# A two-layer mixer: the second weight fold as three fp32r products, its splits on ScalarE and GpSimd, and the first stage's loads and context work put in another order

## The chip, the cores and the metric

The kernel runs on one core of one Trainium2 chip. The time is the device time of one execution in microseconds (us); the times shown are medians of several runs. One more execution was profiled, and every row quoted in this document is from such a profile. The engines are called PE (TensorE, matrix products), DVE (VectorE), ACT (ScalarE), POOL (GpSimd) and SP (SyncE, which issues nearly all DMA transfers). Each engine works through its own list of instructions in a fixed order and waits where an operand isn't there yet.

## The reference

`x` is 1024 tokens of 1024 features, `ctx` 256 tokens that come before them, `c` and `c_ctx` conditioning vectors. Layer 0 (even) and layer 1 (odd) are:

```python
shift, scale, gate = split(silu(c) @ mod_w[l] + mod_b[l], 3)
hx = rmsnorm(x, norm_g[l]) * (1 + scale) + shift
# even layer; hc is ctx under the same weights with c_ctx
va, vg, ga, xb, gb = split(hx @ w_in, 5)
y_a = silu(layernorm(conv31(va * sigmoid(vg)))) * silu(ga)
y_b = rglru(conv4(xb), start=state of rglru(conv4(hc @ w_xb))) * silu(gb)
x = x + gate * (concat(y_a, y_b) @ w_out)
# odd layer
u, g = split(hx @ w_in, 2)
d = multiscale_pool(u)                      # 4 groups of 512 features
y = concat([d_g @ w_grp[g] for g in range(4)]) * od_scale
x = x + gate * ((y * silu(g)) @ w_out)
```

At the end stands one more rmsnorm. The pooling is linear in the tokens, so `u`'s weights and `w_grp` can be multiplied ahead of time: `wu[g] @ grp[g]`, one product of weights for each of the four groups. The kernel calls this a fold.

## The kernel before, in words

Everything is held transposed, features on the 128 partitions and tokens along the free dimension: a tensor of 1024 features is eight tiles (k = 0 to 7) of 128 x 1024. A large product is taken in split precision: an fp32 operand becomes a high part (an fp32r cast on ACT) and a low part (source minus high, on DVE or POOL; `split`, L101), and three products high*high, high*low, low*high are summed in PSUM (`mm3_steps`, L128, and `mm3_fixed`, L487, which also ties the order by hand). A matmul of plain fp32 does without the split; the trace shows it as two records.

The first stage (L293 to L466) does many things at once, and the change lies in it:

- Two of the four folds, `fold_whole` (L267): group matrices `grp[g]` are loaded to two tiles, then four times a tile `wu` is loaded, eight plain fp32 matmuls are made with it (two sums of four), ACT copies each sum (`fo`) and SP stores it to DRAM (`wfold`). `fold_some(n)` (L318) moves on by n steps of this, so the folds are laid between other work.
- The modulation vectors of layer 0: `modulation(k)` (L340) loads two tiles of `mod_w` and DVE multiplies each with silu(c) (`cL`) and silu(c_ctx) (`cC`), summing along the row into `m0`; the products themselves go to a tile `junk` that nobody reads. Two of the eight k are made on PE instead (`mod_row`).
- The rsqrt of x: ACT squares, DVE and POOL add, PE sums over the partitions (L188 to L208).
- `modulate(k)` (L371): DVE multiplies x with the scale and the rsqrt, which lies in PSUM (L375), ACT casts x plus shift to `h0h`, DVE makes `h0l` (L379).
- The context: `ctx_load` (L411) squares on ACT and adds on POOL in pieces of 256 columns, `ctx_scale` (L416) multiplies with the rsqrt on DVE, `modulate_ctx` (L383) applies scale and shift on POOL and splits with POOL.

The stage after it (L705 on) begins with weight tiles `xb0` and `vg0`, the product xb for the context (`xbc`) and for x, and then for each j the products vg, va, xb of the next j, and the gates of the recurrence. Here DVE, ACT, POOL and PE each follow an order written by hand (`on`, L471). The four PSUM buffers of `pm` are taken in turn by vg, va, xbc and the twelve gate products.

Tiles come from pools with a fixed number of buffers per tag; who takes a buffer waits for its last user. Tag `t` has four buffers of 512 columns, the weight tags `wr`, `wh`, `wl` two each of 1024. Where the program doesn't tie the order, a planner lays the instructions of each engine out at build time. In this first stage the loads on SP are tied one after the other (`load`, L108, by `chain`); the stores of the folds are put between them.

Of the kernel before, what the change touches and what calls it, by code (L numbers as in the profile page):

```python
# [15 lines left out]
P = 128  # L16
# [39 lines left out]
def body(ctx, tc, xT, ctxT, cc, ccol, modT, modW, win, gw, wout, wu, grp, wg, wo1, small, edge, ident, outT):  # L56
# [18 lines left out]
    def dtile(name, dt=F32):  # L75
        return dpool.tile([P, S], dt, tag="d", name=name)
# [24 lines left out]
    def split(src, hi, lo, eng):  # L101
        return (nc.scalar.copy(hi, src),  # L102
                eng.tensor_tensor(out=lo, in0=src, in1=hi.bitcast(F32), op=sub))  # L103
# [4 lines left out]
    def load(out, src):  # L108
        with ExitStack() as lctx:
            if chain[0] is not None:  # L110
                lctx.enter_context(tc.issue_after(chain[0].ins))
            d = nc.sync.dma_start(out, src)
            if chain[0] is not None:
                chain[0] = d

    def wload(src, name, eng, n=D, out=None):
        raw = wpool.tile([P, n], F32, tag="wr", name=f"wr_{name}")
        load(raw, src)
        if out is None:
            hi = wpool.tile([P, n], F32R, tag="wh", name=f"wh_{name}")  # L120
            lo = wpool.tile([P, n], F32R, tag="wl", name=f"wl_{name}")
        else:
            hi, lo = out(f"wh_{name}", F32R), out(f"wl_{name}", F32R)
        split(raw, hi, lo, eng)
        return hi, lo
# [15 lines left out]


    sm = base.tile([P, N_SM], F32, name="sm")
    nc.sync.dma_start(sm, small)
    eg = base.tile([P, 4 * 16], F32, name="eg")
    nc.sync.dma_start(eg, edge)

    def col(o, n=1):
        return sm[:, o : o + n]
# [19 lines left out]
    nc.scalar.activation(sa, sa, AF.Exp, scale=-1.0)  # L169
    nc.vector.tensor_scalar(out=sb, in0=sa, scalar1=2.0, scalar2=None, op0=add)  # L170
    nc.vector.reciprocal(sb, sb)
    nc.vector.tensor_tensor(out=sz, in0=sa, in1=sb, op=mult)
    nc.vector.tensor_tensor(out=sb, in0=sz, in1=sz, op=mult)
    nc.vector.memset(sa, 1.0 / 17.0)
    for n in range(7, -1, -1):
        nc.vector.tensor_tensor(out=sa, in0=sa, in1=sb, op=mult)
        nc.vector.tensor_scalar(out=sa, in0=sa, scalar1=1.0 / (2 * n + 1), scalar2=None, op0=add)
    nc.vector.tensor_tensor(out=sa, in0=sa, in1=sz, op=mult)
    nc.vector.tensor_scalar(out=sb, in0=lam, scalar1=-1.0, scalar2=0.0, op0=mult, op1=ALU.max)
    nc.vector.scalar_tensor_tensor(out=sa, in0=sa, scalar=2.0, in1=sb, op0=mult, op1=add)  # L180
    nc.vector.tensor_scalar(out=chalf, in0=sa, scalar1=4.0, scalar2=None, op0=mult)
    nc.vector.tensor_scalar(out=cneg, in0=sa, scalar1=-8.0, scalar2=None, op0=mult)


    def rstd(acc, eps, name, wn=0):
# [78 lines left out]
            yield  # L264


    def fold_whole(g, out_tile, g_tile, w_tile):  # L267
        gs = []
        for i in range(2):
            raw = g_tile(f"graw_{g}_{i}")  # L270
            load(raw, grp[g, i])
            gs += [raw[:, 0:H], raw[:, H:D]]
        yield
        for kp in range(KT // 2):
            w = w_tile(f"wu_{g}_{kp}")
            load(w, wu[g, kp])
            for s in range(2):
                ps = psum(f"fold_{g}_{kp}_{s}")
                for i in range(4):
                    kc = slice(i * 2 * P + s * P, i * 2 * P + (s + 1) * P)  # L280
                    nc.tensor.matmul(ps, w[:, kc], gs[i], start=(i == 0), stop=(i == 3))  # L281
# [15 lines left out]
    hh, hl, ch, cl = [], [], [], []  # L297
    with ExitStack() as sctx:
        fpool = sctx.enter_context(tc.tile_pool(name="fpool", bufs=6))
        gpool = sctx.enter_context(tc.tile_pool(name="gpool", bufs=4))  # L300
        spool = sctx.enter_context(tc.tile_pool(name="spool", bufs=1))

        def fo_tile(name):
            return fpool.tile([P, H], F32, tag="fo", name=name)

        def g_tile(name):
            return gpool.tile([P, D], F32, tag="g", name=name)

        raws = [0]

        def raw_tile(name):
            tag = ("wr", "wh", "wl")[raws[0] % 3]
            raws[0] += 1
            return wpool.tile([P, D], F32, tag=tag, name=name)
# [15 lines left out]
        def sumsq(acc_, v, n, first, name, eng):  # L330
            if first:
                nc.scalar.activation(acc_[:, :n], v, AF.Square)
            else:
                q = ttile(name)
                nc.scalar.activation(q[:, :n], v, AF.Square)
                eng.tensor_tensor(out=acc_[:, :n], in0=acc_[:, :n], in1=q[:, :n], op=add)

        junk = spool.tile([P, D], F32, name="junk")

        def modulation(k):  # L340
            for m in (k, KT + k):
                raw = dtile(f"mod0_{m}")
                load(raw, modT[0, m])
                mod_tile(m0, 0, m, raw, (cL, cC), junk)
            mod_scale(m0, a0, 0, k)

# [36 lines left out]
        def modulate_ctx(k):  # L383
            i, q4 = k // 4, k % 4
            cs = slice(q4 * C, (q4 + 1) * C)
            nc.gpsimd.tensor_scalar(out=cx[i][:, cs], in0=cx[i][:, cs], scalar1=a0[:, 1, k : k + 1],
                                    scalar2=m0[:, 1, k : k + 1], op0=mult, op1=add)
            ch.append(cth[i][:, cs])
            cl.append(ctl[i][:, cs])
            if q4 == 3:  # L390
                split(cx[i], cth[i], ctl[i], nc.gpsimd)

        def x_load(k):
            t = xtile(f"x_{k}")
            load(t, xT[k])
            xs.append(t)
            for h in range(2):
                sumsq(acc[h], t[:, HALF[h]], H, k == 0, f"xsq_{k}_{h}", nc.vector if h else nc.gpsimd)

        for i in range(2):  # L400
            chain[0] = nc.sync.dma_start(cx[i][:1], cc[i : i + 1])
        load(ccv, ccol)
        nc.scalar.activation(ccv, ccv, AF.Silu)
        load(idx, ident)
        for i, t in enumerate((cL, cC)):
            ps = banks(f"c_{i}", i)
            for h in range(2):
# [2 lines left out]
                nc.scalar.activation(t[:, HALF[h]], ps[h], AF.Silu, scale=float(D))  # L410
        def ctx_load(i):  # L411
            load(cx[i].rearrange("p (k n) -> p k n", n=C), ctxT[4 * i : 4 * i + 4].rearrange("k p n -> p k n"))
            for q4 in range(4):
                sumsq(accc, cx[i][:, q4 * C : (q4 + 1) * C], C, i + q4 == 0, f"csq_{i}_{q4}", nc.gpsimd)

        def ctx_scale():  # L416
            rstd(accc, eps_r, "c")
            for i in range(2):
                v = cx[i].rearrange("p (k n) -> p k n", n=C)
                nc.vector.tensor_tensor(out=v, in0=v, in1=accc.unsqueeze(1).to_broadcast([P, 4, C]), op=mult)  # L420

        def ctx_split(i):
            for k in range(4 * i, 4 * i + 4):
                modulate_ctx(k)
# [72 lines left out]
    def all_of(steps):  # L497
        for _ in steps:
            pass
# [127 lines left out]
    with ExitStack() as actx:  # L627
# [1175 lines left out]
```

## Time and profile before

| | |
|---|---|
| time, median of 3 runs | 1308.26 us (1306.17 to 1309.4) |
| the profiled execution's own time | 1307.88 us |
| its span, first to last instruction | 1306.1 us |
| granted TensorE clock, mean | 0.994 |
| first matmul of the first fold | 12.4 us |
| first matmul of the xb product | 82.2 us |
| HBM read, written | 136.72 MB, 44.04 MB |

A timeline row reads: start in us, duration in us, engine, line, operation, tile written<-tiles read, shapes, count (x3: three in a row, the duration is that of all); in brackets the idle time of the engine just before and what ended it. A row of a group ends with: busy us, mean ns of one | idle us before. Buffer numbers are left out of tile names. A busy PE is not PE at its peak, as ends of matmuls are modelled: the distance from one start to the next is what one costs.

### The profile page before, as it was taken

The numbers are of one execution on the slowest core, as the hardware profiler recorded it, in microseconds if no ns is written. First come the engines' busy times: TensorE is split into PE (matmuls) and PEld (weight loads), VectorE is DVE, ScalarE is ACT, GpSimd is POOL, SyncE is SP. The second block draws the span as 40 slices with busy tenths as digits, with TensorE's granted clock in tenths as the row PEclk, the third lists the DMA queues.
The fourth block names the chain that finished last, engine by engine and source line by source line (L and its number), as shares of the span: only waits on it lengthen the run. The fifth ranks groups of instructions, "written<-read, shape, count | busy, mean of one in ns | idle before, by whom it ended". The sixth has DMA issues, their size and how long they took to land.

```text
span 1306.1 us, 15709 instructions
## 1 busy us (share of the span) xinstructions
PE 1276.3 (98%) x5600; PEld 1023.0 (78%) x5600; DVE 1137.2 (87%) x1764; ACT 632.0 (48%) x919; POOL 352.1 (27%) x179
## 2 busy tenths in 40 slices
PE   8999999999999999999999999999999999999995
PEld 3468888888888887788887887788778888778784
DVE  7969999999999989969789758998999987887876
ACT  5333656566656623227435346734343344644642
POOL 2153655576657712443210022000000000000002
PEclk9999999999999999999999999999999999999998
DMA  9934112121112233443555356244334334868723
GB/s 358 360 97 169 57 41 65 41 73 45 61 44 86 65 105 116 152 147 103 169 188 187 127 194 189 86 137 153 109 104 134 113 121 129 284 209 289 265 65 129
DMA packets 82867, 181.80 MB, mean 139 GB/s; under 512 B 7778, under 2 KB 27618, under 8 KB 82788
## 3 DMA queue, kind: packets, MB, share of 16 engines
q1 hardware_dynamic: 74340, 176.60, 40.2%
q10 hardware_dynamic: 8448, 4.20, 1.1%
q8 instruction: 44, 0.72, 0.2%
q14 instruction: 35, 0.29, 0.1%
HBM read 136.72 MB, written 44.04 MB: 138 GB/s over the span
## 4 chain that ended last, share of the span: by engine, by line
PE 68%; DVE 10%; DMA 6%; ACT 4%; issue 2%; POOL 2%; POOLq 0%; SPq 0%; DVEq 0%; ACTq 0%
PE vg L475 7%; PE wob L475 6%; PE xb L475 6%; PE va L475 6%; PE g L475 4%; PE ga L475 2%; PE ga L134 2%; PE ga L133 2%; PE ga L135 2%; PE xbc L475 2%; DVE ws L1340 1%; PE qb_v L963 1%; PE qb_v L966 1%; PE qb_v L965 1%; PE qb_wo L963 1%
## 5 line engine op out<-in xcount | busy, mean ns | idle before, releaser
L475 DVE SCALAR_TENSOR_TENSOR conv<-u,sm,conv 128x505 f32<-128x505 f32 (+6 forms) x224 | 153.8, 746 | 0.9
L1623 POOL TENSOR_TENSOR o<-x,rr 128x256 f32<-128x256 f32 (+1 forms) x9 | 8.1, 931 | 451.1 <-ACT rr L1611 448.1
L475 POOL TENSOR_TENSOR l<-l,l 128x1280 f32<-128x1280 f32 (+1 forms) x23 | 64.0, 2799 | 92.2 <-DVE l L475 65.5
L475 ACT ACTIVATE l<-g,sm 128x512 f32<-128x512 f32 (+1 forms) x96 | 58.7, 619 | 57.8 <-PE g L475 56.0
L281 PE MATMUL fold<-graw,wu 128*128 128x512 f32 x128 | 57.7, 611 | 1.7 <-DMA wu<-wu 1.7
L475 PE MATMUL wob<-ybh,wh_wob 128*128 128x512 f32 x128 | 51.3, 401 | 1.8 <-ACT ybh L475 1.8
L475 DVE TENSOR_TENSOR_SCAN l<-l,l 128x256 f32<-128x256 f32 (+1 forms) x32 | 50.8, 1586 | 1.1
L281 PEld LDWEIGHTS fold<-graw,wu 128*128 128x128 f32 x128 | 24.9, 196 | 33.9 <-issue 29.8
L102 ACT CAST wq_g<-wr_g 128x512 fp32r<-128x512 f32 x48 | 28.3, 621 | 47.6 <-DVE wr_g L944 16.7
L475 PE MATMUL wob<-ybl,wh_wob 128*128 128x512 f32 x128 | 50.9, 397 | 0.4 <-DVE ybl L475 0.4
L475 PE MATMUL wob<-ybh,wl_wob 128*128 128x512 f32 x128 | 50.5, 395 | 0.0
L475 PE MATMUL gb<-h0h,wl_gb 128*128 128x512 f32 x128 | 50.0, 391 | 0.2 <-POOL wl_gb L475 0.2
L475 PE MATMUL vg<-h0h,wl_vg 128*128 128x512 f32 x128 | 50.0, 391 | 0.0
L475 PE MATMUL gb<-h0l,wh_gb 128*128 128x512 f32 x128 | 49.8, 389 | 0.0
L475 PE MATMUL gb<-h0h,wh_gb 128*128 128x512 f32 x128 | 49.8, 389 | 0.0
L475 PE MATMUL vg<-h0h,wh_vg 128*128 128x512 f32 x128 | 49.8, 389 | 0.0
L475 PE MATMUL vg<-h0l,wh_vg 128*128 128x512 f32 x128 | 49.8, 389 | 0.0
L475 PE MATMUL va<-h0h,wh_va 128*128 128x512 f32 x128 | 49.8, 389 | 0.0
L475 PE MATMUL va<-h0l,wh_va 128*128 128x512 f32 x128 | 49.8, 389 | 0.0
L475 PE MATMUL va<-h0h,wl_va 128*128 128x512 f32 x128 | 49.8, 389 | 0.0
L103 POOL TENSOR_TENSOR wl_wu<-wr_wu,wh_wu 128x1024 fp32r<-128x1024 f32 x8 | 19.2, 2400 | 106.4 <-ACT wh_wu L102 105.0
L475 POOL TENSOR_TENSOR l<-l,uc 128x1280 f32<-128x1280 f32 x16 | 47.7, 3006 | 0.0
(602 smaller groups left out, 4314.7 us busy)
## 6 DMA issues: line engine op xcount, KB each, us to landing
mod<-modT SPq DMA_DIRECT2D x20, 512.0 KB, 6.5
x_part<-xp SPq DMA_DIRECT2D x32, 256.0 KB, 2.2
mod<-modT SPq DMA_DIRECT2D x32, 256.0 KB, 3.3
wr_v<-wfold SPq DMA_DIRECT2D x16, 512.0 KB, 3.6
wr_g<-wg SPq DMA_DIRECT2D x16, 512.0 KB, 5.4
wr_wo<-wo SPq DMA_DIRECT2D x16, 512.0 KB, 3.8
y_b<-y SPq DMA_DIRECT2D x24, 256.0 KB, 4.1
y_t<-y SPq DMA_DIRECT2D x24, 256.0 KB, 2.8
```

The lines of the kernel that those rows point to most:

```text
L102: return (nc.scalar.copy(hi, src), eng.tensor_tensor(out=lo, in0=src, in1=hi.bitcast(F32), op=sub))
L103: eng.tensor_tensor(out=lo, in0=src, in1=hi.bitcast(F32), op=sub))
L133: nc.tensor.matmul(ps, hi[:, kc], xh[k][:, cols], start=(k == 0), stop=False)
L134: nc.tensor.matmul(ps, hi[:, kc], xl[k][:, cols], start=False, stop=False)
L135: nc.tensor.matmul(ps, lo[:, kc], xh[k][:, cols], start=False, stop=(k == ks - 1))
L281: nc.tensor.matmul(ps, w[:, kc], gs[i], start=(i == 0), stop=(i == 3))
L475: last[eng] = f(*args, **kw)
L963: nc.tensor.matmul(ps, hi, xh[k], start=(first and k == 0), stop=False, skip_group_check=not first)
L965: nc.tensor.matmul(ps, hi, xl[k], start=False, stop=False, skip_group_check=not first)
L966: mm = nc.tensor.matmul(ps, lo, xh[k], start=False, stop=(k == KH - 1), skip_group_check=not first)
L1340: nc.vector.tensor_tensor(out=nxt[:, :, a_:b_], in0=cur[:, :, a_ + o0 : b_ + o0], in1=cur[:, :, a_ + o1 : b_ + o1], op=add)
L1623: nc.gpsimd.tensor_tensor(out=o[:, k - k0], in0=v, in1=rr, op=mult)
```

## The change

The second fold (group 1) is made by a new `fold_split`: its two group tiles and each half of its `wu` tiles are split by ACT and POOL, and three fp32r matmuls take the place of each fp32 one. The halves of the high and low parts live in the four buffers of tag `t`. Its raw group tiles are loaded to the two context tiles `cx`, which the context itself fills later.

The loads of the small table `sm`, the edge table `eg`, `ccv` and `idx` leave the front of the queue: `sm` comes behind the first `wu`, `ccv` and `idx` behind the last x tile, `eg` far later. The decay rates (27 small operations on DVE, two on ACT) are made after the context's second split. The context's squares are made in pieces of 1024 columns into `junk` and `cC`; its scale, shift and low parts move from POOL to DVE; the weights `xb0` and `vg0` are loaded and split ahead of it. The product xbc for j = 0 comes behind the first half of vg instead of at the head, and xb leaves k = 7 of both halves for last. The second fold's last step comes ahead of the context's scale; before, it was left to the stage's end.

```diff
-    nc.sync.dma_start(sm, small)
     eg = base.tile([P, 4 * 16], F32, name="eg")
-    nc.sync.dma_start(eg, edge)
...
-    nc.scalar.activation(sa, lam, AF.Abs)
...
+    def decay_rates():
+        nc.scalar.activation(sa, lam, AF.Abs)
...
+    def fold_split(g, out_tile, raws, g_high, g_low, w_tile, half_tile):
+        gs = []
+        for i in range(2):
+            hi, lo = g_high[i](f"gh_{g}_{i}", F32R), g_low[i](f"gl_{g}_{i}", F32R)
+            load(raws[i], grp[g, i])
+            split(raws[i], hi, lo, nc.gpsimd)
+            gs += [(hi[:, h], lo[:, h]) for h in HALF]
+        yield
+        for kp in range(KT // 2):
+            raw = w_tile(f"wu_{g}_{kp}")
+            load(raw, wu[g, kp])
+            pss = [psum(f"fold_{g}_{kp}_{s}") for s in range(2)]
+            for n in range(2):
+                hi, lo = half_tile(f"wh_{g}_{kp}_{n}"), half_tile(f"wl_{g}_{kp}_{n}")
+                split(raw[:, HALF[n]], hi, lo, nc.gpsimd)
+                for s in range(2):
+                    ps = pss[s]
+                    for i in range(2):
+                        gh, gl = gs[2 * n + i]
+                        kc = slice(i * 2 * P + s * P, i * 2 * P + (s + 1) * P)
+                        nc.tensor.matmul(ps, hi[:, kc], gh, start=(n + i == 0), stop=False)
+                        nc.tensor.matmul(ps, hi[:, kc], gl, start=False, stop=False)
+                        nc.tensor.matmul(ps, lo[:, kc], gh, start=False, stop=(n + i == 2))
+            for s in range(2):
...
-        gpool = sctx.enter_context(tc.tile_pool(name="gpool", bufs=4))
+        gpool = sctx.enter_context(tc.tile_pool(name="gpool", bufs=5))
...
-        folds = (u for g in range(2) for u in fold_whole(g, fo_tile, g_tile, raw_tile))
...
+        def half_tile(name):
+            return tpool.tile([P, H], F32R, tag="t", name=name)
+
+        tags = iter(("wr", "wl", "wh", "wr", "wr", "wl", "wl", "wr"))
...
+        def both_folds():
+            yield from fold_whole(0, fo_tile, g_tile, raw_tile)
+            yield from fold_split(1, fo_tile, cx, (g_tile, g_tile), (g_tile, g_high), raw_tile, half_tile)
...
-            nc.gpsimd.tensor_scalar(out=cx[i][:, cs], in0=cx[i][:, cs], scalar1=a0[:, 1, k : k + 1],
+            nc.vector.tensor_scalar(out=cx[i][:, cs], in0=cx[i][:, cs], scalar1=a0[:, 1, k : k + 1],
                                     scalar2=m0[:, 1, k : k + 1], op0=mult, op1=add)
...
-                split(cx[i], cth[i], ctl[i], nc.gpsimd)
+                cast_ = split(cx[i], cth[i], ctl[i], nc.vector)[0]
...
-            for q4 in range(4):
-                sumsq(accc, cx[i][:, q4 * C : (q4 + 1) * C], C, i + q4 == 0, f"csq_{i}_{q4}", nc.gpsimd)
+            q = (junk, cC)[i]
+            nc.scalar.activation(q, cx[i], AF.Square)
+            q = [q[:, n * C : (n + 1) * C] for n in range(4)]
+            if i == 0:
+                nc.gpsimd.tensor_tensor(out=accc, in0=q[0], in1=q[1], op=add)
+                q = q[2:]
+            for v in q:
+                nc.gpsimd.tensor_tensor(out=accc, in0=accc, in1=v, op=add)
...
+        def first_weights():
+            fold_some(1)
+            load(sm, small)
 
         fold_some(1)
-        modulation(0)
-        fold_some(1)
+        modulation(0, first_weights)
...
         x_load(7)
+        load(ccv, ccol)
+        nc.scalar.activation(ccv, ccv, AF.Silu)
+        load(idx, ident)
...
         ctx_load(0)
-        fold_some(1)
+        fold_some(2)
         ctx_load(1)
         ctx_scale()
+        wxb = wload(win[3 * KT], "xb0", nc.gpsimd)
+        wvg = wload(win[KT], "vg0", nc.gpsimd)
         ctx_split(0)
-        ctx_split(1)
-        fold_some(10)
+        with tc.issue_after(ctx_split(1).ins):
+            decay_rates()
...
-        w = wload(win[3 * KT], "xb0", nc.gpsimd)
-        xc = psum("xbc0")[:, :C]
+        w = wxb
         xb = wide("xb0")
-        mm3(xc, w, (ch, cl), slice(0, C))
-        for h in range(2):
-            mm3(xb[:, HALF[h]], w, (hh, hl), HALF[h])
-        w = wload(win[KT], "vg0", nc.gpsimd)
-        uc = utile("uc0")
-        first_tap(0, xc, uc[:, :C])
-        other_taps(0, xc, uc[:, :C])
+        steps = [mm3_steps(xb[:, HALF[h]], w, (hh, hl), HALF[h]) for h in range(2)]
+        for n in (KT - 1, 1):
+            for x in steps:
+                for _ in range(n):
+                    next(x)
+        w = wvg
...
             all_of(mm3_fixed(vg[0], w, (hh, hl), HALF[0]))
             if state is not None:
                 rec_input(state, 1)
+            else:
+                xc = psum("xbc0")[:, :C]
+                all_of(mm3_fixed(xc, wxb, (ch, cl), slice(0, C)))
+                uc = utile("uc0")
+                first_tap(0, xc, uc[:, :C])
+                other_taps(0, xc, uc[:, :C])
...
     nc.sync.dma_start(idD, ident)
+    nc.sync.dma_start(eg, edge)
```

More of the change, by code (lines that the diff above doesn't have):

```diff
@@ L167, in body @@
     sz = base.tile([P, NL], F32, name="sz")
-    nc.scalar.activation(sa, lam, AF.Abs)
[L169 to L182, printed above, removed]
+    def decay_rates():
+        nc.scalar.activation(sa, lam, AF.Abs)
+        nc.scalar.activation(sa, sa, AF.Exp, scale=-1.0)
+        nc.vector.tensor_scalar(out=sb, in0=sa, scalar1=2.0, scalar2=None, op0=add)
+        nc.vector.reciprocal(sb, sb)
+        nc.vector.tensor_tensor(out=sz, in0=sa, in1=sb, op=mult)
+        nc.vector.tensor_tensor(out=sb, in0=sz, in1=sz, op=mult)
+        nc.vector.memset(sa, 1.0 / 17.0)
+        for n in range(7, -1, -1):
+            nc.vector.tensor_tensor(out=sa, in0=sa, in1=sb, op=mult)
+            nc.vector.tensor_scalar(out=sa, in0=sa, scalar1=1.0 / (2 * n + 1), scalar2=None, op0=add)
+        nc.vector.tensor_tensor(out=sa, in0=sa, in1=sz, op=mult)
+        nc.vector.tensor_scalar(out=sb, in0=lam, scalar1=-1.0, scalar2=0.0, op0=mult, op1=ALU.max)
+        nc.vector.scalar_tensor_tensor(out=sa, in0=sa, scalar=2.0, in1=sb, op0=mult, op1=add)
+        nc.vector.tensor_scalar(out=chalf, in0=sa, scalar1=4.0, scalar2=None, op0=mult)
+        nc.vector.tensor_scalar(out=cneg, in0=sa, scalar1=-8.0, scalar2=None, op0=mult)
     def rstd(acc, eps, name, wn=0):
@@ L264, in fold @@
             yield
+    def fold_split(g, out_tile, raws, g_high, g_low, w_tile, half_tile):
[22 more added lines that the diff above has]
+            for s in range(2):
+                dst = wfold[g][:, :, 2 * kp : 2 * kp + 2, :]
+                o = out_tile(f"fo_{g}_{kp}_{s}")
+                nc.scalar.copy(o, pss[s])
+                nc.sync.dma_start(dst[:, :, s, :].rearrange("m p c -> p m c"),
+                                  o.rearrange("p (m c) -> p m c", c=P))
+            yield
     def fold_whole(g, out_tile, g_tile, w_tile):
@@ L304, in fo_tile, with g_tile, g_high, raw_tile @@
             return fpool.tile([P, H], F32, tag="fo", name=name)
[L306 to L314, printed above, removed]
-        folds = (u for g in range(2) for u in fold_whole(g, fo_tile, g_tile, raw_tile))
+        def g_tile(name, dt=F32):
+            return gpool.tile([P, D], dt, tag="g", name=name)
+        def g_high(name, dt):
+            return wpool.tile([P, D], dt, tag="wh", name=name)
+        def half_tile(name):
+            return tpool.tile([P, H], F32R, tag="t", name=name)
+        tags = iter(("wr", "wl", "wh", "wr", "wr", "wl", "wl", "wr"))
+        def raw_tile(name, dt=F32):
+            return wpool.tile([P, D], dt, tag=next(tags), name=name)
+        def both_folds():
+            yield from fold_whole(0, fo_tile, g_tile, raw_tile)
+            yield from fold_split(1, fo_tile, cx, (g_tile, g_tile), (g_tile, g_high), raw_tile, half_tile)
+        folds = both_folds()
         def fold_some(n):
@@ L338, in body, with modulation @@
         junk = spool.tile([P, D], F32, name="junk")
-        def modulation(k):
+        def modulation(k, between=lambda: None):
+            raws_ = []
             for m in (k, KT + k):
-                raw = dtile(f"mod0_{m}")
-                load(raw, modT[0, m])
+                raws_.append(dtile(f"mod0_{m}"))
+                load(raws_[-1], modT[0, m])
+            between()
+            for m, raw in zip((k, KT + k), raws_):
                 mod_tile(m0, 0, m, raw, (cL, cC), junk)
@@ L390, in modulate_ctx @@
             if q4 == 3:
-                split(cx[i], cth[i], ctl[i], nc.gpsimd)
+                cast_ = split(cx[i], cth[i], ctl[i], nc.vector)[0]
+            return cast_ if q4 == 3 else None
         def x_load(k):
@@ L401, in body @@
             chain[0] = nc.sync.dma_start(cx[i][:1], cc[i : i + 1])
-        load(ccv, ccol)
-        nc.scalar.activation(ccv, ccv, AF.Silu)
-        load(idx, ident)
         for i, t in enumerate((cL, cC)):
@@ L423, in ctx_split @@
             for k in range(4 * i, 4 * i + 4):
-                modulate_ctx(k)
+                c = modulate_ctx(k)
+            return c
+        def first_weights():
+            fold_some(1)
+            load(sm, small)
         fold_some(1)
-        modulation(0)
-        fold_some(1)
+        modulation(0, first_weights)
         x_load(0)
```

## The prediction

> **What bounds the kernel now.** I read the page's busy shares first, then the busy time by stretch, because every edit lies in the first 125 us.
>
> ```profile
> PE 1276.3 (98%) x5600; PEld 1023.0 (78%) x5600; DVE 1137.2 (87%) x1764; ACT 632.0 (48%) x919; POOL 352.1 (27%) x179
> ```
>
> Columns below: PE, weight loads, DVE, ACT, POOL busy us (count), granted clock, DMA share, GB/s.
>
> ```profile
> 9.80:27.20 17.40, 15.68 (x32) 6.56 (x31) 14.10 (x17) 10.44 (x19) 8.10 (x6) 1.00 1.03 411
> 27.20:81.20 54.00, 53.49 (x158) 24.49 (x158) 52.95 (x90) 22.81 (x37) 13.41 (x9) 1.00 0.84 297
> 81.20:98.80 17.60, 17.36 (x85) 14.07 (x84) 4.05 (x4) 4.17 (x6) 12.31 (x11) 1.00 0.26 76
> 300.00:400.00 100.00, 100.00 (x479) 84.23 (x478) 98.58 (x127) 62.54 (x72) 66.16 (x28) 1.00 0.19 64
> ```
>
> PE is full from its first fold on, so a microsecond less on PE is a microsecond less at the end, if its operands keep up. But DVE is full too from 27 to 81 us (52.95 of 54.0), rests only from 81 to 99, and is as full as PE later on (98.6 of 100 against 100.0). Two engines are bound at once; the timeline and two pieces of the chain of waits (without operands) tell which one waits for the other.
>
> ```profile
> 12.40 22.95 PE L281 MATMUL fold<-graw,wu 128*128 128x512 f32 x48 [1.72 <-DMA wu<-wu]
> 47.72 27.73 PE L281 MATMUL fold<-graw,wu 128*128 128x512 f32 x64
> 77.56 3.67 DVE L379 SCALAR_TENSOR_TENSOR h0l<-x,m,h0h 128x1024 fp32r<-128x1024 f32 x3
> 82.19 0.79 PE L133 MATMUL xb<-h0h,wh_xb 128*128 128x512 f32 x1
> 88.07 0.39 PE L133 MATMUL xb<-h0h,wh_xb 128*128 128x512 f32 x1
> 88.75 0.39 PE L133 MATMUL xb<-h0h,wh_xb 128*128 128x512 f32 x1
> 98.04 0.40 PE L475 MATMUL vg<-h0h,wl_vg 128*128 128x512 f32 x1
> 98.20 9.77 PE vg L475 x43
> 118.85 2.87 PE xbc L475 x24
> 119.54 1.29 DVE L475 TENSOR_TENSOR u<-va,sg 128x512 f32<-128x512 f32 x2
> 122.62 0.40 PE L475 MATMUL g<-uh,wh_gw 128*128 128x512 f32 x1
> ```
>
> PE finishes the folds and begins xb at 82.19; DVE delivers the last three h0l tiles (k = 5, 6, 7) at 81.23. A step of xb is three matmuls and 0.68 us. From here on I call the end of the last h0l Th.
>
> **The change part by part: PE.** One fp32 matmul of a fold is two records, 64 records in 27.73 us, so 0.43 us each. The second fold is 64 records, 27.6 us. As three products it is 32 x 3 matmuls at 0.68/3 = 0.227 us, 21.8 us: minus 5.8. The front of the SP queue:
>
> ```profile
> 0.74 0.39 SPq L144 DMA_DIRECT2D sm<-small  x1
> 1.18 0.42 SPq L146 DMA_DIRECT2D eg<-edge  x1
> 1.65 0.59 SPq L401 DMA_DIRECT2D cx<-cc  x2
> 2.29 0.36 SPq L112 DMA_DIRECT2D ccv<-ccol  x1
> 2.69 0.43 SPq L112 DMA_DIRECT2D idx<-ident  x1
> 3.17 0.90 SPq L112 DMA_DIRECT2D graw<-grp  x2
> sm<-small SPq DMA_DIRECT2D x1, 224.0 KB, 2.6
> ```
>
> Four issues leave the front: 0.91 us ahead of cx and 0.88 ahead of graw, 1.8 together for the first weights. The small table then lies between wu and x: 224 KB at the 411 GB/s of the stretch is 0.56, so the x tiles, and DVE, gain 1.2. ccv and idx move behind x7 and are first wanted past 36 us; the edge table is wanted by the pooling stage alone; both at nothing. PE is tied to DVE once before 48 us (the rsqrt of x), so it keeps 1.2 there. It could begin xb at 82.2 - 1.2 - 5.8 = 75.2.
>
> **DVE, and what GpSimd does to it.** The splits are new: on ACT two casts of 1024 and eight of 512 columns (about 7 us; ACT is busy 22.8 of 54, so it covers them), on POOL the same ten as subtractions, in just the stretch where DVE is full.
>
> ```profile
> 29.78 1.27 POOL L336 TENSOR_TENSOR ssq<-ssq,xsq 128x512 f32<-128x512 f32 x1 [2.98 <-ACT xsq L335]
> 29.79 1.27 DVE L223 TENSOR_TENSOR m<-m,sm 128x2 f32<-128x2 f32 x1
> 33.99 0.16 DVE L223 TENSOR_TENSOR m<-m,sm 128x2 f32<-128x2 f32 x1
> 62.43 2.71 DVE L375 SCALAR_TENSOR_TENSOR x<-x,a,ms_x 128x512 f32<-128x512 f32 x4
> 63.17 2.35 POOL L336 TENSOR_TENSOR ssqc<-ssqc,csq 128x256 f32<-128x256 f32 x3
> 66.61 1.73 DVE L379 SCALAR_TENSOR_TENSOR h0l<-x,m,h0h 128x1024 fp32r<-128x1024 f32 x1
> 68.89 3.33 POOL L103 TENSOR_TENSOR wl_xb<-wr_xb,wh_xb 128x1024 fp32r<-128x1024 f32 x1
> 69.94 3.36 DVE L379 SCALAR_TENSOR_TENSOR h0l<-x,m,h0h 128x1024 fp32r<-128x1024 f32 x1
> L103 POOL TENSOR_TENSOR wl_vg<-wr_vg,wh_vg 128x1024 fp32r<-128x1024 f32 x1 | 2.4, 2389 | 0.0
> L375 DVE SCALAR_TENSOR_TENSOR x<-x,a,ms_x 128x512 f32<-128x512 f32 x16 | 10.8, 741 | 0.3 <-PE ms_x L207 0.3
> ```
>
> The same 128x2 addition takes 0.16 alone and 1.27 beside a POOL operation of 1.27: it stands still for all of it. An h0l tile takes 1.22 (three in 3.67) and 3.36 while POOL splits wl_xb: 2.1 lost. Only x<-x,a,ms_x, whose second input is in PSUM, goes on at full speed beside POOL's additions (four in 2.71). So a split costs DVE its own length, unless it falls on the 10.8 us of x<-x. On POOL the ten are 2 x 2.39 + 8 x 1.27 = 14.9 us. Bounds: nothing (all under x<-x or in DVE's idle time, 1.05 us here), and 14.9. The two raw tiles of the second fold and its first wu half should arrive at 38 to 45 us, where six x<-x run; the later halves come one per 2.7 us of PE, and one or two of them meet x<-x. I take 9 lost, nearer the upper bound.
>
> The Trainium skill, "SBUF — State Buffer", section "Who interferes with whom", states this as a rule: a VectorE instruction with two SBUF inputs and a GpSimd instruction that reads SBUF exclude one another, for a whole instruction. The trace agrees (1.27 against 0.16), also in the PSUM exception (2.71 for four). By the rule the splits cost VectorE what is summed here; were GpSimd's work free beside it, the result would be the faster rival below.
>
> The context's seven additions on POOL hinder DVE now: an h0l tile beside one takes 1.73 in place of 1.22, 0.5 each; three fall on x<-x, four make 2.0. Their squares move into junk and cC, which the modulation uses to its end, so all seven come behind the last modulation product, where six x<-x follow; I leave 0.7 for one or two that miss them: minus 1.3. Together
>
> Th = 81.2 - 1.2 + 9 - 1.3 = 87.7.
>
> **PE again.** From 75.2 PE does k = 0 to 4 (3.4 us) and then stands at k = 5 with the rest of xb, vg and the context product queued behind it. k = 6 is ready at Th - 1.2 = 86.5; then 1 + 7 + 2 steps of 0.68 (the new order leaves k = 7 of both halves for last) end at 93.3, half a vg (24 x 0.227 = 5.4) at 98.7, a context product (24 in 2.87) at 101.6. Before, xb, the context product and 5 of vg's 48 (43 are left in the chain of waits) were done at 98.04; 19 more make 102.4. So of 7 us won PE keeps 0.8. The other 6.2 go to the wait for h0l.
>
> **DVE behind Th.** Two pieces move into its 13.6 us of rest:
>
> ```profile
> 3.85 0.17 DVE L170 TENSOR_SCALAR sb<-sa 128x16 f32<-128x16 f32 x1 [0.21 <-ACT sa L169]
> 8.63 0.17 DVE L182 TENSOR_SCALAR cneg<-sa 128x16 f32<-128x16 f32 x1
> 81.14 1.75 DVE L191 RECIPROCAL ssqc<-sq_c 128x256 f32<-128x256 f32 x1
> 82.93 2.36 DVE L420 TENSOR_TENSOR cx<-cx,ssqc 128x1024 f32<-128x1024 f32 x2
> 98.89 1.52 DVE L475 SCALAR_TENSOR_TENSOR uc<-xbc,sm,uc 128x254 f32<-128x254 f32 x3 [13.60 <-ACT uc L475]
> L475 DVE SCALAR_TENSOR_TENSOR uc<-xbc,sm,uc 128x255 f32<-128x255 f32 x4 | 1.9, 483 | 0.1
> L475 DVE SCALAR_TENSOR_TENSOR l<-l,cL 128x1024 f32<-128x1024 f32 x8 | 15.3, 1971 | 0.0
> ```
>
> Context: reciprocal and scaling 1.75 + 2.4 as now; eight shifts of 256 columns, not in the trace on DVE, between 0.17 (128x16) and 0.48 (128x255 with PSUM), a quarter of a cx row gives 0.3, so 2.4; two subtractions like cx rows, 2.4. Decay rates: 3.85 to 8.80, 5.0. Sum 14.0: DVE is free at 101.7, just as the context product ends. (If PE's order puts the context's mean square behind the waiting xb step, the reciprocal is a little later than Th; the range holds that.) The taps begin 0.85 behind it (98.04 to 98.89), at 102.5, and from them to the end of the first u half it is 98.89 to 120.2 = 21.3 as now, POOL's splits in it included (the eight l<-l,cL take 1.97 against 1.22): 123.8. The second gate product on PE takes the PSUM buffer of the first va half and so waits for that u; now it starts at 122.62 with 2.4 us to spare, then at 123.8. So the change costs 1.2, and behind it both engines go on as now.
>
> The profiled execution took 1307.9 with a span of 1306.1; 1.2 more is 1309.1. The median shown is 0.4 above that execution: **1309**. A measurement of this kernel can tell 0.3% (3.9 us) from no change.
>
> **The rivals.** *The splits find room on DVE* (they fall on x<-x, or POOL's part is done while DVE waits). With at most 2 us lost, Th is 80.7; PE goes from 75.2 without a stop through xb, half vg and the context product: 94.4. Taps at 95.3, u at 116.6, against 122.6: minus 6, **1302**. For it: PE order and h0 tiles fit to a few tenths then. Against it: DVE has 1 us of idle time in 54.
>
> *Slower: none of the ten subtractions falls on x<-x.* Then 14.9 are lost, Th = 93.6, 5.9 later than forecast, and everything behind Th moves with it: plus 7.1, **1315**. It decides from 11.7 lost on. For it: x<-x is 10.8 of 54 us, and POOL also splits wvg in this stretch, which now falls into DVE's rest. Against it: six x<-x in a row stand where the first splits come. A smaller dose of it is the forecast.
>
> The Trainium skill, "TensorE: Matmul & The Clock Gate", Part 1, has the array at half rate after an idle window of about 3.4 us; a stop of 6 us ahead of xb would then add about 2 us on PE (an estimate from that page: half of one window). The first fold's matmuls are 0.86 apart until 16.7 us, which agrees.
>
> *The ring paces the fold.* The halves live in four small buffers, so a cast and a subtraction must fit into the 2.7 us that PE takes for the other half: 0.6 + 1.27, and up to 1.2 of waiting for DVE. If this eats all of the 5.8, PE begins xb at 81.0; k = 6 is then reached at 85.1, still ahead of 86.5: **1309** again. The change then does not give what it says, and nothing is seen of it.
>
> **How the numbers follow.** Forecast with the ring case 0.45; splits find room 0.32; all blocked 0.23. These are also the chances of same, faster and slower. Loss on DVE from 0 to about 13 gives 1301 to 1313; the rest of the blocked case lies above.
>
> **What would show it.** Right: h0l<-x,m,h0h at two to three times 1.22 beside POOL's wl of the second fold; PE idle before an xb step, released by DVE h0l; the last h0l past 85. Wrong: PE passing from the fold into xb by 77 without a stop and h0l done by 82; or idle time of PE inside the fold longer than that ahead of xb.

## The result, and the profile after

The change makes the kernel slower: 1314.86 us (median of 6 runs, 1313.6 to 1318.42) against 1308.49 (6 runs of the kernel before beside them, 1303.49 to 1309.4), ratio 1.0063 with a 95% interval of 1.0047 to 1.0079. The profiled execution took 1318.42 with a span of 1316.6 and a mean granted clock of 0.988, against a span of 1306.1 and 0.994 before. It is the longest of the six; I use it for waits and durations, and the ratios of medians for verdicts.

How late PE is can be read from the start of a product in both timelines (start, duration), before and then after the change. For later use the fence of before also shows the first g product; gb is the first product behind the eight j:

```profile
121.56 0.28 PE L475 MATMUL g<-uh,wh_gw 128*128 128x256 f32 x1
...
416.76 0.40 PE L475 MATMUL gb<-h0h,wh_gb 128*128 128x512 f32 x1
```

```profile
425.59 0.40 PE L531 MATMUL gb<-h0h,wh_gb 128*128 128x512 f32 x1
```

8.8 us of the 10.5 by which the spans differ have arisen by here. I call this distance the lag. The busy time by stretch after the change, the stretches and columns as in the prediction, and PE's waits between 27 and 140 us (times in total, count, longest):

```profile
27.20:81.20 54.00, 47.37 (x175) 27.84 (x173) 53.40 (x83) 23.58 (x36) 24.86 (x13) 0.97 0.77 276
81.20:98.80 17.60, 16.90 (x74) 13.89 (x75) 13.63 (x18) 7.29 (x11) 10.00 (x7) 1.00 0.34 104
```

```profile
PE fold L287 <- ACT wh L102: 3.9, 3, 1.6
PE g L531 <- DVE u L531: 3.7, 1, 3.7
PE fold L289 <- POOL wl L103: 2.6, 3, 1.4
```

From 27 to 81 us DVE is as full as before (53.4), but PE now has 47.4 of 54 where it had 53.5: it stands inside the split fold, 6.5 us in all, and again at the second gate product. PE's timeline has the split fold's first matmul, three from its middle, and the xb steps in and behind it:

```profile
52.94 0.79 PE L287 MATMUL fold<-gh,wh 128*128 128x512 f32 x1
...
70.27 0.79 PE L289 MATMUL fold<-gh,wl 128*128 128x512 f32 x1 [0.77 <-POOL wl L103]
70.86 0.63 PE L287 MATMUL fold<-gh,wh 128*128 128x512 f32 x1
71.29 0.63 PE L288 MATMUL fold<-gl,wh 128*128 128x512 f32 x1
...
82.94 0.40 PE L133 MATMUL xb<-h0h,wh_xb 128*128 128x512 f32 x1
...
88.20 0.39 PE L133 MATMUL xb<-h0h,wh_xb 128*128 128x512 f32 x1
```

From 52.94 to 88.20, without the 3.4 us of five xb steps laid in it, the split fold takes PE 31.8 us, where 21.8 were forecast and the plain fold takes 27.7. The waits are 6.5 of the 10.0 that this is too long; 1.4 more are lost behind the wait at 70.27, where matmuls stand 0.43 us apart in place of 0.227; the rest lies at the edges of the waits, whose idle time counts only from the modelled end of the matmul before.

DVE's timeline shows where its own time went:

```profile
48.54 2.27 DVE L422 SCALAR_TENSOR_TENSOR h0l<-x,m,h0h 128x1024 fp32r<-128x1024 f32 x1
...
60.68 1.12 DVE L223 TENSOR_TENSOR m<-m,sm 128x2 f32<-128x2 f32 x1
...
73.46 3.42 DVE L422 SCALAR_TENSOR_TENSOR h0l<-x,m,h0h 128x1024 fp32r<-128x1024 f32 x1
...
82.70 4.96 DVE L422 SCALAR_TENSOR_TENSOR h0l<-x,m,h0h 128x1024 fp32r<-128x1024 f32 x3
91.60 1.75 DVE L191 RECIPROCAL ssqc<-sq_c 128x256 f32<-128x256 f32 x1 [3.94 <-ACT sq_c L190]
93.39 2.36 DVE L467 TENSOR_TENSOR cx<-cx,ssqc 128x1024 f32<-128x1024 f32 x2
95.67 2.67 DVE L429 TENSOR_SCALAR cx<-cx,a,m 128x256 f32<-128x256 f32 x8
98.26 2.43 DVE L103 TENSOR_TENSOR ctl<-cx,cth 128x1024 fp32r<-128x1024 f32 x2
...
105.26 0.48 DVE L531 SCALAR_TENSOR_TENSOR uc<-xbc,sm,uc 128x254 f32<-128x254 f32 x1 [0.74 <-ACT uc L531]
...
107.89 1.89 DVE L176 TENSOR_TENSOR sa<-sa,sb 128x16 f32<-128x16 f32 x1
...
127.83 1.28 DVE L531 TENSOR_TENSOR u<-va,sg 128x512 f32<-128x512 f32 x2
```

The h0l tiles of 1.22 us take 2.27 and 3.42 and an addition of 128x2 takes 1.12, as the forecast had it. Th, the end of the last h0l, is 82.70 + 4.96 = 87.66. Behind it DVE stands 3.94 us for the context's rsqrt, whose sum POOL completes only at 89.90 (timeline of POOL):

```profile
84.99 4.91 POOL L461 TENSOR_TENSOR ssqc<-ssqc,cC 128x256 f32<-128x256 f32 x4
```

The taps begin at 105.26 and u comes at 127.83, where it came at 119.54 before. PE pays for that here (timeline of PE):

```profile
123.68 0.28 PE L531 MATMUL g<-uh,wh_gw 128*128 128x256 f32 x1
...
128.56 0.80 PE L531 MATMUL g<-uh,wh_gw 128*128 128x512 f32 x1 [3.67 <-DVE u L531]
129.16 0.63 PE L531 MATMUL g<-ul,wh_gw 128*128 128x512 f32 x1
...
134.65 0.39 PE L531 MATMUL xb<-h0h,wl_xb 128*128 128x512 f32 x1
```

The first g product is 2.1 later than before (121.56). Then comes a stop of 3.67. Then the fourteen matmuls from 128.56 to 134.65 take 6.09 us, where 14 x 0.227 = 3.2 were due: they run at half rate (granted clock 0.83 from 120 to 140 us, 1.00 before), 2.9 lost. 2.1 + 3.7 + 2.9 = 8.7, the lag. The first two come to the same thing as the second g product's start: 128.56, in place of 122.62 before.

### The profile page after: what moved, and what is told of

It is laid out like the page before. It is cut to its first block, busy times and chain, and to the rows that moved or that the text cites. A ratio compares the mean times of both kernels' runs of the same rounds, so it can differ in the third digit from the quotient of the medians.

```text
span 1316.6 us, 15787 instructions
## 1 busy us (share of the span) xinstructions
PE 1278.5 (97%) x5632; PEld 1032.5 (78%) x5632; DVE 1151.4 (87%) x1774; ACT 636.7 (48%) x923; POOL 359.6 (27%) x179
## 5 line engine op out<-in xcount | busy, mean ns | idle before, releaser
L531 DVE SCALAR_TENSOR_TENSOR conv<-cL,wsum,conv 128x506 f32<-128x506 f32 (+3 forms) x70 | 47.5, 744 | 0.2
L102 ACT CAST wq_v<-wr_v 128x512 fp32r<-128x512 f32 x48 | 28.2, 620 | 36.7 <-DMA wr_v<-wfold 13.9
```

The source lines that it names most:

```text
L102: return (nc.scalar.copy(hi, src), eng.tensor_tensor(out=lo, in0=src, in1=hi.bitcast(F32), op=sub))
L531: last[eng] = f(*args, **kw)
```

## The experiments

Ratios are to the kernel before, run on the same chip beside each. Times of one kernel spread by up to 11 us.

**1. The change without the split fold.**

```diff
-            yield from fold_split(1, fo_tile, cx, (g_tile, g_tile), (g_tile, g_high), raw_tile, half_tile)
+            yield from fold_whole(1, fo_tile, g_tile, raw_tile)
```

> The second fold is plain fp32 again (8 fp32 matmuls for each wu tile, no splits); everything else of the change stays. Theory: the loss comes from the ten subtractions on POOL, which hold DVE up and, through ACT's order, PE. Without them the last h0l ends near 78.7 us (87.7 less 9), the context's sum is there when DVE asks for it, and the half of vg now ahead of the context product puts the taps at about 101: no stop of PE over 1 us, 1307 to 1309 us. Rival: the loss comes from the work laid behind the last h0l (context on DVE, decay rates, context product a gate later). Then u stays as late as after the change and the time is 1313 to 1315.

1307.54 us, ratio 1.0006 (0.9997 to 1.0015): no difference that can be measured. Its DVE timeline:

```profile
72.91 5.61 DVE L422 SCALAR_TENSOR_TENSOR h0l<-x,m,h0h 128x1024 fp32r<-128x1024 f32 x3 [0.39 <-ACT h0h L421]
84.50 1.75 DVE L191 RECIPROCAL ssqc<-sq_c 128x256 f32<-128x256 f32 x1 [5.98 <-ACT sq_c L190]
```

Th is 78.52, 9.1 earlier than with the splits: the 9 us "lost" of the prediction, measured. DVE's wait for the rsqrt is longer here (5.98) and costs nothing, since the taps wait for PE's context product anyway. Two points of the expectation missed: the context's sum isn't there when DVE asks for it, and PE still stops 1.8 us at the second gate product. All of the loss hangs on the split fold.

**2. The context's squares in buffers of their own.**

```diff
-            q = (junk, cC)[i]
+            q = g_tile(f"csq_{i}")
```

> The context's squares go to two buffers of the group tiles, free once the first fold is done, in place of junk and cC, so that POOL can add them before the last splits. Theory: DVE's idle time behind the last h0l (3.94 us, waiting for the context's sum) goes, u comes about 4 us earlier, PE's stop of 3.67 us and the 3.05 us of half clock behind it go: 1307 to 1309. Rival: DVE is late by POOL's splits alone and the idle time is only slack; the additions now stop h0l instead, the last h0l ends 2 us later, and the time stays at 1313 to 1315.

1322.18, ratio 1.0109 (1.0096 to 1.0123): my theory fell, and the rival's number was passed too. POOL's last additions, PE's stop and its product for the rsqrt (timelines of POOL, then PE):

```profile
80.22 0.73 POOL L461 TENSOR_TENSOR ssqc<-ssqc,csq 128x256 f32<-128x256 f32 x1
```

```profile
82.51 0.79 PE L133 MATMUL xb<-h0h,wh_xb 128*128 128x512 f32 x1 [4.77 <-DVE x L418]
...
93.10 0.59 PE L188 MATMUL ms_c<-ssqc,ones 128*128 128x256 f32 x2
```

The context's sum is complete at 80.95, ahead of the last h0l (86.33), yet DVE waits 8.7 us for the rsqrt. The product ms_c stands in PE's fixed order behind xb and the fold's last step, and PE stood 4.8 us there for DVE: in this build the wait runs in a ring from DVE over PE's order back to DVE. In the changed kernel itself it was the additions that came last (89.90, with ms_c right behind at 90.46). The planner laid several engines out differently in this build, so it tells nothing on the additions' own cost.

**3. The halves' subtractions on DVE.**

```diff
-                split(raw[:, HALF[n]], hi, lo, nc.gpsimd)
+                split(raw[:, HALF[n]], hi, lo, nc.vector)
```

> The eight subtractions of the wu halves run on DVE instead of POOL. Theory: a subtraction on POOL holds DVE up for its own length (1.1 to 1.2 us each), on DVE it costs half a h0l, 0.6 us. DVE gets 5 us more of its own work and loses 8 to 9 us of standing still: the last h0l ends at 84 to 86 in place of 87.7, the context's additions on POOL come in one run, DVE's idle time of 3.94 shrinks to under 2, and the time is 1307 to 1311. Rival: POOL's work is free for DVE. Then 5 us are simply added, the last h0l ends at 92 to 93 and the time is 1317 to 1320.

1308.61, ratio 1.0012 (1.0000 to 1.0023). From its DVE timeline, and POOL's beside it:

```profile
66.64 0.69 DVE L103 TENSOR_TENSOR wl<-wu,wh 128x512 fp32r<-128x512 f32 x1
67.24 1.28 DVE L422 SCALAR_TENSOR_TENSOR h0l<-x,m,h0h 128x1024 fp32r<-128x1024 f32 x1
...
71.38 2.91 DVE L103 TENSOR_TENSOR wl<-wu,wh 128x512 fp32r<-128x512 f32 x1
...
80.24 3.67 DVE L422 SCALAR_TENSOR_TENSOR h0l<-x,m,h0h 128x1024 fp32r<-128x1024 f32 x3
85.97 4.56 DVE L467 TENSOR_TENSOR cx<-cx,ssqc 128x1024 f32<-128x1024 f32 x2
```

```profile
70.60 3.15 POOL L103 TENSOR_TENSOR wl_xb<-wr_xb,wh_xb 128x1024 fp32r<-128x1024 f32 x1 [26.30 <-ACT wh_xb L102]
```

Giving DVE eight operations more makes it earlier: Th is 83.91 in place of 87.66. A half costs 0.69 on DVE itself. When POOL does it DVE stands still for about 1 us (after the change, the h0l of 2.27 is 1.05 over its 1.22). Eight times 0.69 is 5.5 us more of its own work, and Th is 3.7 earlier all the same: some 9.2 us of standing still are gone. Where POOL still works (wl_xb), a DVE subtraction of 0.69 takes 2.91. The rival, that POOL's work is free beside DVE, would have had Th at 92 and is out.

The Trainium skill, "SBUF — State Buffer", section "Summary: rules for kernel authors", says that where VectorE has two SBUF inputs while a GpSimd operation reads SBUF, the one that issues second fully blocks until the first is done. Experiments 1 and 3 agree with it in the sum over a stage (9.1 and some 9.2 us).

**4. Six buffers for the halves.** The second halves go to two group tiles, free after the first fold.

```diff
-                hi, lo = half_tile(f"wh_{g}_{kp}_{n}"), half_tile(f"wl_{g}_{kp}_{n}")
+                ht = half_tiles[n]
+                hi, lo = ht(f"wh_{g}_{kp}_{n}"), ht(f"wl_{g}_{kp}_{n}")
```

> The second halves of the split wu tiles get buffers of their own (two group tiles free after the first fold), six buffers for the halves in place of four. Theory: the casts are late because they stand behind h0h in ACT's order, which waits for DVE; more buffers leave more than half of PE's 6.5 us of waits inside the fold, and what PE wins there it loses again at u: 1312 to 1316. Rival: the four buffers pace the fold. Then PE's waits inside the fold fall under 1.5 us, xb begins near 77 and the time falls to 1309 or less.

1313.14, ratio 1.0055 (1.0038 to 1.0072), as the theory had it. PE still waits 5.1 us in the fold (4.0 + 0.7 + 0.4) of 6.5, and 3.66 at g. So the four buffers are not the main thing that paces the fold. That they have no part in it isn't shown: Th is 85.17 here, xb begins at 79.95 and gb at 421.14, a lag of 4.4. But the profiled execution is the fastest of its six (1308.49), and the medians don't tell this kernel from the changed one. ACT's timeline after the change shows the main wait:

```profile
66.60 1.15 ACT L421 ACTIVATE h0h<-x,m 128x1024 fp32r<-128x1024 f32 x1 [5.96 <-DVE x L418]
67.65 0.60 ACT L102 CAST wh<-wu 128x512 fp32r<-128x512 f32 x1
...
80.19 1.15 ACT L421 ACTIVATE h0h<-x,m 128x1024 fp32r<-128x1024 f32 x1 [3.62 <-DVE x L418]
81.25 0.60 ACT L102 CAST wh<-wu 128x512 fp32r<-128x512 f32 x1
```

The casts stand behind h0h in ACT's order, and h0h waits 5.96 and 3.62 us for DVE's x. Two of PE's three waits for a cast end right behind these (at 68.31 and 81.90). That is read from the rows; no run has another order of ACT.

**5. u ahead of three of the products l<-l,cL.** DVE's order alone is changed; the same work is done.

```diff
-                for m in range(2 * KT, 3 * KT):
+                gate_mod(range(2 * KT, 3 * KT - 3))
...
             for h in range(2):
...
                 vec(nc.vector.tensor_tensor, out=u[:, HALF[h]], in0=ps, in1=sg[h], op=mult)
+            if state is None:
+                gate_mod(range(3 * KT - 3, 3 * KT))
```

> The changed kernel with one thing moved: three of the eight products l<-l,cL on DVE (and the small sum behind them) come behind the two u instead of ahead of them. Nothing is left out. Theory: the second gate product waits for u alone, which stands behind these products in DVE's order. u comes 5.7 us earlier (three times 1.9), PE's stop of 3.7 us at g and the 3.0 us of half clock behind it go: 1306 to 1309. Rival: DVE itself sets the end from here on, and PE's stop is only where that shows first. Then the stop turns up again at a later place and the time stays at 1312 to 1316.

1314.31, ratio 1.0052 (1.0035 to 1.0069): the rival. The stop at g is gone, u comes 3.5 earlier (124.29), and a later stop takes its place (timeline of PE):

```profile
188.18 0.50 PE L531 MATMUL vg<-h0h,wl_vg 128*128 128x512 f32 x1 [2.77 <-POOL wl_vg L531]
...
189.50 0.63 PE L531 MATMUL vg<-h0l,wh_vg 128*128 128x512 f32 x1
189.92 0.63 PE L531 MATMUL vg<-h0h,wl_vg 128*128 128x512 f32 x1
```

with half rate behind it again. POOL's wl_vg stood there behind an l<-l, for which POOL had waited 14.49 us for DVE. The lag at gb is 7.3 (424.03). DVE is late by its amount of work; where PE notices it is a matter of order.

**6. The decay rates at the front again.**

```diff
             load(sm, small)
+            decay_rates()
...
-        with tc.issue_after(ctx_split(1).ins):
-            decay_rates()
+        ctx_split(1)
```

> The decay rates are made at the front again, right behind the load of the small table; everything else of the change stays. Theory: behind the last h0l DVE is free of 5 us, of which some 3 to 4 lie among the taps; at the front DVE has 3 us of rest before 27 us, so the last h0l is 0 to 2 us later. u comes 2 to 4 us earlier, PE's stop at g shrinks from 3.7 to under 1.5: 1308 to 1312. Rival: what DVE gets rid of there only lengthens its wait for the context product, which PE delivers late: 1313 to 1316.

1314.69, ratio 1.0060 (1.0045 to 1.0075). The rival held, its wait for the context product grown from 0.7 to 4.6. The theory also had Th wrong: it comes 3.8 later (91.48). DVE had 3.3 us of rest from 9.8 to 27.2 us after the change (busy 14.11 of 17.4), but the decay rates fill only 1.4 of it (15.51); the first x<-x begins at 43.06 in place of 39.93. Where the decay rates stand makes no difference to the time that can be measured.

**7. The split fold alone.** The kernel before with `fold_split` and its buffers, nothing else of the change.

```diff
-        folds = (u for g in range(2) for u in fold_whole(g, fo_tile, g_tile, raw_tile))
+            yield from fold_whole(0, fo_tile, g_tile, raw_tile)
+            yield from fold_split(1, fo_tile, cx, (g_tile, g_tile), (g_tile, g_high), raw_tile, half_tile)
```

> The kernel before with the split fold alone: loads at the front, decay rates at the front, context on POOL and its product ahead of vg as before. Theory: the ten subtractions on POOL carry the whole loss: the last h0l ends at 88 to 91 in place of 81.2, PE stops in the fold or ahead of xb for 5 us or more, 1312 to 1318. Rival: the split fold is harmless by itself and loses only together with the work that the change puts behind the last h0l: 1305 to 1309.

1315.96, ratio 1.0068 (1.0053 to 1.0083). PE's waits from 50 to 120 us:

```profile
PE fold L287 <- ACT wh L102: 4.1, 1, 4.1
PE xb L133 <- DVE x L415: 3.5, 1, 3.5
PE fold L289 <- POOL wl L103: 2.3, 2, 1.3
PE vg L515 <- POOL wl_vg L103: 0.8, 1, 0.8
```

The split fold loses as much alone as with the rest. So the other parts (load order, decay rates, context) neither cause the loss nor repair it. Here PE does stop ahead of xb, but not as I forecast it: it stops ahead of the first step, not at k = 5, and what releases it (at 84.58) is DVE's last x<-x, not an h0l.

**8. Experiments 3 and 5 together**, the two edits shown there.

> The fold's subtractions of the halves on DVE (as in the third experiment) and u ahead of three of the products l<-l,cL (as in the fifth). Theory: without the stop of 1.7 us at g PE keeps the 1.5 us that it is ahead of the kernel before when it reaches va: 1304 to 1306, or 0.999 of before. Rival: DVE has as much to do as PE until the end of the stage, so the 1.5 us are lost at the next wait for DVE: 1307 to 1309.

1306.49, ratio 0.9999 (0.9987 to 1.0011): between the two ranges in us, but no gain is left, as the rival had it. The stretch from 120 to 240 us, first of the kernel before, then of this one:

```profile
120.00:240.00 120.00, 120.00 (x575) 100.87 (x574) 117.55 (x166) 72.53 (x85) 67.31 (x27) 1.00 0.15 47
```

```profile
120.00:240.00 120.00, 118.89 (x563) 99.34 (x563) 118.73 (x171) 72.27 (x85) 67.52 (x27) 1.00 0.14 49
```

Before, PE had no rest at all and DVE 2.4 us. Here PE rests 1.1 (a wait for POOL's wl_vg, which stands behind an l<-l as in experiment 5) and DVE 1.3. The lead of 1.3 us that PE has at the first g product (120.30) is gone at gb (416.92).

**9. Also the subtractions of xb0 and vg0 on DVE.**

```diff
-        wxb = wload(win[3 * KT], "xb0", nc.gpsimd)
-        wvg = wload(win[KT], "vg0", nc.gpsimd)
+        wxb = wload(win[3 * KT], "xb0", nc.vector)
+        wvg = wload(win[KT], "vg0", nc.vector)
```

> The kernel of the eighth experiment, with the subtractions of the weights xb0 and vg0 on DVE too, so that POOL has only the context's seven additions between 45 and 92 us. Theory: DVE is what sets the end, and a subtraction on POOL costs it more than one of its own. In the eighth experiment two DVE operations took 3.4 us in place of 1.2 beside the two subtractions; on DVE these are 1.2 each. DVE gains 2.0, PE keeps its 1.3: 1304 to 1306, 0.998 to 0.999 of before. Rival: DVE is not the bound here, then nothing changes against the eighth experiment: 1306 to 1307.5.

1305.80, ratio 0.9989 (0.9980 to 0.9999): faster than both kernels, by little, with an interval that just leaves out 1. gb begins at 415.25, 1.5 ahead of before. Again DVE is earlier with more work on it: u begins at 117.19, in experiment 8 at 118.90. But this build also has the whole fold ahead of xb (its last matmul at 78.61, in experiment 8 at 85.27), so the gain isn't shown to come from the two subtractions alone.

**10. One more k of the modulation on PE** (on top of 9).

```diff
-KD = 6
+KD = 5
...
-        modulation(5)
```

> The ninth experiment with one more of the eight k of the modulation made on PE (three in place of two): DVE loses four products of 1.22 us, PE's row products get 384 columns in place of 256, 16 times 0.21 = 3.4 us more. Theory: DVE sets the end, and PE's stops in the fold and ahead of xb (5.2 us in the eighth experiment) are waits for DVE that shrink with it. PE nets 0 to 2 us, DVE 5: 1302 to 1305. Rival: PE sets the end as much as DVE, so its 3.4 us are paid in full: 1307 to 1310.

1313.97, ratio 1.0056 (1.0037 to 1.0076): worse than either expected. DVE gets into one long wait:

```profile
87.74 0.69 DVE L103 TENSOR_TENSOR wl<-wu,wh 128x512 fp32r<-128x512 f32 x1 [5.99 <-ACT wh L102]
```

```profile
86.40 0.59 ACT L293 COPY fo<-fold 128x512 f32<-128x512 f32 x1 [7.33 <-PE fold L289]
```

ACT's cast stands behind this copy of the fold's sum, for which ACT waited 7.33 us: in this build PE has most of xb ahead of the fold's last steps. What KD = 5 is worth with another order stays open.

**11. No split fold, with the edits of 5 and 9.**

> The first experiment (second fold in plain fp32, no splits) with u ahead of three of the products l<-l,cL and the subtractions of xb0 and vg0 on DVE. Theory: DVE is early here, PE has its full 27.6 us of fold: PE is 1.3 ahead of before when it reaches va, and keeps it once u no longer stops it: 1304 to 1306. Then the three products of the split fold bring nothing even where DVE is helped as far as here. Rival: the fold's 5.8 us on PE are a real gain once DVE has room: then this is 1 to 3 us slower than the ninth experiment.

1307.02, ratio 0.9995 (0.9982 to 1.0008), 0.06% behind experiment 9, within both intervals. By the medians it is 1.2 us slower than experiment 9, which lies in the rival's range and outside the theory's; the intervals decide for neither. The fold's three products save PE 5.8 us on paper. Even where DVE has been helped, some 1 us of it is seen, and that isn't certain.

## Why the prediction was wrong, point by point

- **The lock between POOL and DVE, and Th: right.** Forecast 9 lost, Th 87.7; measured 87.66, and 78.52 with the fold unsplit, 9.1 apart. That Th agrees to a tenth is luck: the loads brought DVE 1.7 in place of 1.2 (its first x<-x begins at 39.93, before at 41.67), and that made up for additions of the context that cost more than the 0.7 I left (in experiment 1, without splits, the last three h0l took 5.61 in place of 3.67).
- **"It could begin xb at 75.2" and "then stands at k = 5": wrong in place.** PE never waited for h0l; it stood 6.5 us inside the fold, and xb began at 82.94. That the stops in the fold are longer than that ahead of xb is one of the signs of being wrong that the prediction names. xb could not have begun at 75.2 in any case: its tile takes the PSUM buffer in which the rsqrt of one half of x lies (tag `xb`, one buffer), so it waits for DVE's last x<-x. That ends at 82.79 here, and in nine of the ten kernels with the split fold xb begins within 0.2 us of it. By the prediction's own steps this costs little (sixteen of 0.68 from 82.94 end at 93.8, forecast 93.3), so it isn't what the time is off by.
- **"ACT is busy 22.8 of 54, so it covers them": wrong.** I had put a stop in the fold down to the ring of four buffers and bounded it at 5.8. The buffers aren't the main cause (experiment 4). The casts queue behind h0h, and through ACT's order DVE's lateness reaches PE. The prediction didn't ask what stands ahead of the casts in ACT's order.
- **"Sum 14.0: DVE is free at 101.7": mis-sized.** The context's work itself took 9.1 (91.60 to 100.69), as forecast. But the parenthesis "a little later than Th", put at nothing in the sum, was 3.94: four of the seven additions on POOL fell beside the last h0l tiles and ended 2.2 us behind Th, where I had all but one or two beside the six x<-x. And nine of the decay rates' operations fell among the taps and the products l<-l,cL, one of them 1.89 long beside POOL. Taps 105.26 against 102.5, end of the first u half 128.5 against 123.8.
- **"The change costs 1.2": the step that failed.** The second gate product waits for u, as the prediction says, but it began at 128.56 in place of 123.8, 4.8 late by the terms just named, and 2.9 of half rate came on top: 1.2 + 4.8 + 2.9 = 8.9, the lag but for 0.1. I had priced half rate for the stop ahead of xb alone, in a sentence beside the sum; behind g I left it out, though the sum itself has PE standing there (0.8 early at a product that comes 1.2 late). The stop at g by itself would have looked avoidable; experiment 5 shows that moving u alone doesn't gain it.
- **"Behind it both engines go on as now": wrong as a reason.** Both engines are full there, so a stage that ends late on DVE wasn't made up on PE (experiments 5 and 8).
- **The rivals.** The slower one gave 1315 through Th = 93.6, with all ten subtractions blocking. The time fits by luck: Th was 87.66. Room for the splits on DVE (1302) did not exist. "The ring paces the fold" saw the right place and named what isn't the main cause, and I let it end without cost.

What stays open: how the 6.5 us in the fold divide between ACT's order and POOL's own waiting for DVE. PE's waits name ACT for 3.9 and POOL for 2.6; no run parts them. And the one profiled execution is 10.5 longer than that of before, where the medians differ by 6.4. Of its 10.5, 1.7 arise behind 425 us, where the change edits next to nothing: from 1140 to 1160 us its granted clock is 0.91, before 1.00, and eight matmuls stand 0.43 apart behind waits of 1.29 and 0.93 us, which loses 1.6. How often such stretches come in the other five executions isn't known.

## What to carry to other kernels

Before moving an elementwise operation from a full VectorE, or a new one, to GpSimd, ask what VectorE does meanwhile: here a subtraction cost VectorE about 1 us of standing still from GpSimd and 0.69 on VectorE itself, and with subtractions taken back VectorE was earlier, in experiments 3 and 9. Where two engines are full in a stage, don't expect a saving on one to be worth more than the other's rest there (2.4 us of 120 here). And for work put on an idle engine, look at what it queues behind: an engine busy for 23 of 54 us still delivered late, by its rows because its order tied the new work to the fullest engine.

## What the runs showed of the hardware

A stop of PE can be paid twice. After the stop of 3.67 us matmuls of 512 columns were 0.43 apart for 6.1 us, in experiment 4 after a stop of 3.66 for only 2.7 us (125.58 to 128.30), and in experiment 5 after a stop of 2.77 us from 189.5 to 192.5. Two short waits close together did it too: in the changed kernel's fold waits of 1.65 and 0.77 us, which end at 68.31 and 70.27, are followed by matmuls 0.43 apart until 73.0. After the single stop of 1.8 us in experiment 1 they stayed 0.23 apart.

The Trainium skill, "TensorE: Matmul & The Clock Gate", Part 1, says that half rate follows on an idle window of about 3.4 us and that these windows run free of the program. The two lengths behind equal stops agree with the second. With the first the measurement differs, and decides: stops shorter than 3.4 us were enough.
